# Where combination pieces and weight loads stand in the order of a gated S5 and dilated-attention block

## The chip, the core and the metric

The kernel runs on one core of one Trainium2 chip. The metric is the time of one execution in device microseconds, as the median of three runs. The engines are TensorE (PE for its matmuls, PEld for its weight loads), VectorE (DVE), ScalarE (ACT), GpSimd (POOL) and SyncE (SP); SP issues the DMAs that matter here, in one queue.

## The reference, cut to what matters

One layer on x of 2048 x 1024 in float32. A normalised h is multiplied by one wide matrix and split into the inputs of a state-space branch (u, z_s), queries, keys and values of 12 heads (3 groups of 4), a gate z_a, and two merge gates.

```python
proj = rmsnorm(x, pre_norm_g) @ w_in
u_s, z_s, q, k, v, z_a, g_s, g_a = split(proj)
y_s = s5_branch(u_s, ...) * silu(z_s)
# three groups (window, dilation) = (128,1), (512,4), (2048,16), four heads each
outs, lses = [dilated_group_attention(q_g, k_g, v_g) for g in range(3)]
alpha = softmax(lses over the three groups)      # per head slot j
y_a = sum(alpha * outs) * silu(z_a)
merged = sigmoid(g_s) * (y_s @ w_branch_s) + sigmoid(g_a) * (y_a @ w_branch_a)
x = x + rmsnorm(merged @ w_out, post_norm_g)
```

A head slot j has one head in each of the three groups. Its outputs are mixed by `alpha`, which needs the softmax sums of all three.

## The kernel before, in words

Every float32 operand of a large product is split into a rounded high part and a remainder (`split`: ACT writes the high part, DVE the low part), and a product is three matmuls (high x high, high x low, low x high). h lies split in on-chip memory for all of the first part of the program.

Weights come in pairs of 128-column strips. `pair` takes a pair of tiles from the pool `wp` (two pairs of buffers, so two pairs of strips can be held) and loads four parts of 256 KB through tiles of the tag `w_raw`, of which there are two. `proj` multiplies one strip with 512 columns of h in 24 matmuls: one bank.

The stages in order are: normalisation and the first products, the state-space branch with gate and value products beside it, the GLU, and then attention. Attention runs over four head slots j, and in each over three units, one for each group g (`unit`). A unit has one weight pair (query and key strip), and four chunks of 512 positions. A chunk projects keys and queries, loads its values from DRAM (tile `ev` for the banded groups g = 0 and 1, which ACT and DVE then split into `vh`, `vl`; tile `v` for g = 2, used as it comes), computes scores, softmax (tile `p`: DVE maximum, ACT exponential), transposes p on TensorE and multiplies with the values; the unnormalised result goes to DRAM (`numd`), the softmax sums go to `statd`.

After a slot's three units, `combine(j)` mixes its three outputs. It is a Python generator that is advanced one piece at a time beside later work. Its first piece loads the sums (`cm`), works out the three factors on DVE and ACT and stores them (`fd`). Then come eight pieces, one for each quarter and half: for each of the three groups a broadcast of the factor and a block of `numd` are loaded into one `w_raw` tile (there named `cnf`), GpSimd multiplies and adds them into the tile `cy`, and the sum goes to DRAM (`yad`). So combination and weight loads share the two `w_raw` tiles. GpSimd also copies two carried key blocks for each later chunk of a g = 0 unit.

Pieces of slot j are called for in slot j+1, after chunks 0, 1 and 3 of each unit (`if c != 2: next(beside, None)`), nine calls for nine pieces. Those of the last slot are called for after the banks of `emit(tanh(0), beside)` and `emit(tanh(2), beside)`, the first two pairs of merge-gate products. Then follow the z_a strips (`silu_pair`, whose results are multiplied by the combined output, loaded into `cy` tiles of the pool `za`) with `tanh(4)` between them, `tanh(6)`, and the loads of the first halves of both branch weights (`wbs`, `wba`), the first inputs of the last stage (`branch_inputs`) and its first gates. The last stage (`output`) runs over eight blocks of 256 positions: branch products (`br`), merge, output product (`po`), normalisation.

The program text isn't the order on the engines. [...] Tiles of one tag are handed out in the order of the text.

Of the kernel before, what the change touches and what calls it, by code (L numbers as in the profile page):

```python
# [11 lines left out]
F32 = mybir.dt.float32  # L12
# [27 lines left out]
class Builder:  # L40
# [783 lines left out]
    def unit(self, j, g, wp, pool, ev, psum, numd, statd, beside):  # L824
        nc = self.nc
        banded = g < 2
        w = self.pair(wp, IDX_Q + 4 * g + j, IDX_K + 4 * g + j)
        st = pool.tile([128, 2, 16], F32, name="st", bufs=2)
        prev = None
        for c in range(4):  # L830
            view = self.chunk(g, c)

            def project(s):
                ps = psum.tile([128, 512], F32, tag="proj", name="proj")
                self.proj(ps, w, s, view)
                return self.in_order(g, ps)

            vsrc = self.vd[g, 512 * c : 512 * c + 512, 128 * j : 128 * j + 128].rearrange("(b q) x -> q b x", b=4)
            pk = project(1)
            if banded:  # L840
                vh, vl = (pool.tile([128, 4, 128], F32R, name=n, bufs=2) for n in ("vh", "vl"))
                self.load_split(ev, "ev", vh, vl, vsrc)
                kh, kl = (pool.tile([128, 5, 128], F32R, name=n, bufs=2) for n in ("kh", "kl"))
                flat = lambda t: self.ordered(g, t.rearrange("p b i -> p (b i)"))
                self.split(flat(kh[:, 1:5]), flat(kl[:, 1:5]), pk)
                carry = g == 0 and c > 0
                if carry:
                    nc.gpsimd.tensor_copy(kh[:, 0], prev[0][:, 4])
                    nc.gpsimd.tensor_copy(kl[:, 0], prev[1][:, 4])
                pq = project(0)  # L850
                qh, ql = (pool.tile([128, 4, 128], F32R, name=n) for n in ("qh", "ql"))
                self.split(flat(qh), flat(ql), pq)
                self.banded_chunk(g, c, carry, qh, ql, kh, kl, vh, vl, prev, st, pool, ev, psum, numd[j, g, c])
                prev = (kh, kl, vh, vl)
            else:
                v = pool.tile([128, 4, 128], F32, tag="vh", name="v", bufs=2)
                nc.sync.dma_start(v, vsrc)
                k = pool.tile([128, 4, 128], F32, tag="kh", name="k", bufs=2)
                nc.scalar.activation(k.rearrange("p b i -> p (b i)"), pk, AF.Copy)
                pq = project(0)  # L860
                q = pool.tile([128, 4, 128], F32, tag="qh", name="q")
                nc.scalar.activation(q.rearrange("p b i -> p (b i)"), pq, AF.Copy)
                self.causal_chunk(c, q, k, v, st, pool, ev, psum, numd[j, g, c])
            if c != 2:
                next(beside, None)

        tp = psum.tile([32, 128], F32, tag="t", name="tst")
        nc.tensor.transpose(tp, st.rearrange("p s b -> p (s b)"), self.ident)
        sb = pool.tile([32, 128], F32, name="stt")
        if g == 0:  # L870
            nc.vector.tensor_copy(sb.rearrange("s (r i) -> s r i", r=16), tp.rearrange("s (i r) -> s r i", r=16))
            for s in range(2):
                nc.sync.dma_start(
                    statd[j, g, s].rearrange("(r b i) -> b r i", r=16, b=16),
                    sb[16 * s : 16 * s + 16].rearrange("s (r i) -> s r i", r=16),
                )
        elif g == 1:
            nc.vector.tensor_copy(sb.rearrange("s (m i) -> s m i", m=4), tp.rearrange("s (i m) -> s m i", m=4))
            for s in range(2):
                for c in range(4):  # L880
                    nc.sync.dma_start(
                        statd[j, g, s].rearrange("(m r b i) -> r b m i", m=4, r=4, b=4)[c],
                        sb[16 * s + 4 * c : 16 * s + 4 * c + 4].rearrange("s (m i) -> s m i", m=4),
                    )
        else:
            nc.vector.tensor_copy(sb, tp)
            nc.sync.dma_start(statd[j, g].rearrange("s (r i) -> (s r) i", r=16), sb)
# [102 lines left out]
    def combine(self, j, wp, pool, numd, statd, fd, yd):  # L990
# [2 lines left out]
        nc = self.nc  # L993
        m = pool.tile([128, 6, 16], F32, name="cm")
        nc.sync.dma_start(m, statd[j].rearrange("g s (p x) -> p (g s) x", x=16))
        mx = pool.tile([128, 16], F32, name="cx")
        nc.vector.tensor_tensor(mx, m[:, 0], m[:, 2], op=ALU.max)
        nc.vector.tensor_tensor(mx, mx, m[:, 4], op=ALU.max)
# [13 lines left out]
        for q in range(4):  # L1012
            for o in (0, 256):
                y = pool.tile([128, 256], F32, name="cy")
                for g in range(3):
                    r = wp.tile([128, 2, 256], F32, tag="w_raw", name="cnf", bufs=2)
                    f, n = r[:, 0], r[:, 1]
# [118 lines left out]
    def run(self, stop=None):  # L1136
        tc, nc, a = self.tc, self.nc, self.a
        with (
# [8 lines left out]
            ya = self.ya = dp.tile([4, 4, 128, 512], F32, name="ya")  # L1147
# [11 lines left out]
            T = dict(reuse_waits="tile")  # L1159
# [5 lines left out]
            with tc.tile_pool(name="w", bufs=2, **T) as wp, tc.tile_pool(name="ev", bufs=2, **T) as ev:  # L1165
# [37 lines left out]
                with tc.tile_pool(name="at", bufs=1, **T) as ap:  # L1203
                    self.mask = ap.tile([128, 256], F32, name="mask")
                    nc.sync.dma_start(self.mask, a["mask"])

                    beside = iter(())
                    for j in range(4):
                        for g in range(3):
                            self.unit(j, g, wp, ap, ev, psum, numd, statd, beside)  # L1210
                        beside = self.combine(j, wp, ap, numd, statd, fd, yad)
                    if stop == "att":
                        return

                    def tanh(c):
                        w = self.pair(wp, IDX_GA + c, IDX_GA + c + 1)
                        return self.tanh_pair(ev, psum, w, gta[c : c + 2])

                    def emit(banks, beside=iter(())):
                        for bank in banks:  # L1220
                            for step in bank:
                                step()
                            next(beside, None)

                    emit(tanh(0), beside)
                    emit(tanh(2), beside)
                with tc.tile_pool(name="za", bufs=1, **T) as zp:

                    def mixed(j, q):
                        f = zp.tile([128, 512], F32, name="cy", bufs=3)  # L1230
                        nc.sync.dma_start(f, yad[j, q])
                        return f

                    for p in range(2):
                        if p:
                            emit(tanh(4))
                        i = IDX_ZA + 2 * p
                        factor = [lambda q, j=j: mixed(j, q) for j in (2 * p, 2 * p + 1)]
                        emit(self.silu_pair(ev, psum, self.pair(wp, i, i + 1), ya[2 * p : 2 * p + 2], factor))
                if stop == "ya":  # L1240
                    return
                with tc.tile_pool(name="bs", bufs=1, **T) as bp:
                    emit(tanh(6))
                    wb = [self.weight(bp, wp, "w_raw", n, 4, (0, 512)) for n in ("wbs", "wba")]
                    first = self.branch_inputs(wp, 0, 256, ys, ya)
                    early = [bp.tile([128, 2, 256], F32, name="gt", bufs=2) for _ in range(2)]
                    for c, gt in enumerate(early):
                        self.gates(gt, c, 0)
                    hcm.__exit__(None, None, None)
                    with tc.tile_pool(name="out", bufs=1, side="right", **T) as op:  # L1250
                        self.output(op, bp, wp, ev, psum, wb, first, early, ys, ya, 256)
# [56 lines left out]
```

## Time and profile before

| | |
|---|---|
| Median of three runs | 2163.32 us (2162.99 to 2163.49) |
| The profiled execution's own time | 2165.62 us |
| Its span, first to last instruction | 2163.8 us |
| Mean granted TensorE clock | 0.983 |
| TensorE matmul busy | 2062.1 us, 95% of the span |
| VectorE, ScalarE, GpSimd busy | 41%, 27%, 19% of the span |
| HBM traffic | 106 GB/s over the span |

TensorE is the engine that is nearly always busy, so time is read from the stretches in which it is not, and from those in which its granted clock is below 1. The other engines matter where TensorE waits for them.

### The profile page before, as it was taken

The numbers are of one execution on the slowest core, as the hardware profiler recorded it, in microseconds if no ns is written. First come the engines' busy times: TensorE is split into PE (matmuls) and PEld (weight loads), VectorE is DVE, ScalarE is ACT, GpSimd is POOL, SyncE is SP. The second block draws the span as 40 slices with busy tenths as digits, with TensorE's granted clock in tenths as the row PEclk, the third lists the DMA queues.
The fourth block names the chain that finished last, engine by engine and source line by source line (L and its number), as shares of the span: only waits on it lengthen the run. The fifth ranks groups of instructions, "written<-read, shape, count | busy, mean of one in ns | idle before, by whom it ended". The sixth has DMA issues, their size and how long they took to land.

```text
span 2163.8 us, 31149 instructions
## 1 busy us (share of the span) xinstructions
PE 2062.1 (95%) x11668; PEld 1790.3 (83%) x11668; DVE 879.6 (41%) x2293; ACT 587.1 (27%) x1327; POOL 413.3 (19%) x464
## 2 busy tenths in 40 slices
PE   8999999999999999998998999899399999999998
PEld 6788888999999988876886787778378878899987
DVE  6981456555522244243323423341012125554435
ACT  6421122222223234232323323332021124211211
POOL 0002455555402100023003201300400001111111
PEclk9999999999999999999999999999799999999999
DMA  7333343343345411135115313421543247343323
GB/s 258 107 119 127 104 123 116 117 121 110 114 135 170 133 49 52 35 98 136 57 50 134 112 40 90 128 78 54 131 132 117 88 122 219 103 143 117 122 78 98
DMA packets 237239, 239.85 MB, mean 111 GB/s; under 512 B 48160, under 2 KB 177952, under 8 KB 236832
## 3 DMA queue, kind: packets, MB, share of 16 engines
q1 hardware_dynamic: 237088, 237.87, 36.5%
q8 instruction: 91, 1.49, 0.3%
q14 instruction: 60, 0.49, 0.1%
HBM read 150.65 MB, written 78.75 MB: 106 GB/s over the span
## 4 chain that ended last, share of the span: by engine, by line
PE 76%; DMA 13%; POOL 3%; DVE 3%; ACT 2%; issue 2%; SPq 1%; DVEq 0%; POOLq 0%; ACTq 0%
PE proj L141 40%; PE pv L163 12%; PE br L1092 7%; PE po L1111 7%; DMA cnf<-numd 4%; PE glu L786 2%; DMA w_raw<-in_wst_dram 2%; DMA yad<-cy 1%; DMA ev<-vd 1%; POOL cnf L1032 1%; DMA cnf<-fd 1%; POOL cy L1033 1%; PE s L917 1%; DMA raw<-in_wout_dram 1%; PE py L598 1%
## 5 line engine op out<-in xcount | busy, mean ns | idle before, releaser
L141 PE MATMUL proj<-hhi,w_hi 128*128 128x512 f32 x1664 | 665.6, 401 | 45.2 <-ACT w_hi L67 35.8
L141 PE MATMUL proj<-hlo,w_hi 128*128 128x512 f32 x1664 | 662.0, 398 | 3.8 <-DVE hlo L68 2.7
L141 PE MATMUL proj<-hhi,w_lo 128*128 128x512 f32 x1664 | 661.0, 398 | 0.0
L141 PEld LDWEIGHTS proj<-hhi,w_hi 128*128 128x128 f32 x1664 | 316.4, 190 | 115.3 <-ACT w_hi L67 36.3
L141 PEld LDWEIGHTS proj<-hlo,w_hi 128*128 128x128 f32 x1664 | 316.6, 190 | 72.5 <-DVE hlo L74 3.4
L141 PEld LDWEIGHTS proj<-hhi,w_lo 128*128 128x128 f32 x1664 | 316.4, 190 | 62.5
L163 PE MATMUL pv<-w_hi,hhi 128*128 128x256 f32 x768 | 218.8, 285 | 0.0
L163 PE MATMUL pv<-w_hi,hlo 128*128 128x256 f32 x768 | 214.5, 279 | 0.0
L163 PE MATMUL pv<-w_lo,hhi 128*128 128x256 f32 x768 | 214.5, 279 | 0.0
L68 DVE TENSOR_TENSOR w_lo<-w_raw,w_hi 128x512 fp32r<-128x512 f32 (+1 forms) x130 | 107.9, 848 | 256.0 <-ACT w_hi L67 255.5
L1095 POOL TENSOR_TENSOR gt<-gt 128x256 f32<-128x256 f32 x64 | 48.7, 764 | 504.9 <-DVE gt L1094 344.3
L163 PEld LDWEIGHTS pv<-w_hi,hhi 128*128 128x128 f32 x768 | 144.4, 188 | 0.6
L163 PEld LDWEIGHTS pv<-w_lo,hhi 128*128 128x128 f32 x768 | 144.4, 188 | 0.6
L163 PEld LDWEIGHTS pv<-w_hi,hlo 128*128 128x128 f32 x768 | 144.3, 188 | 0.0
L900 ACT ACTIVATE p<-p,nm 128x128 f32<-128x128 f32 (+1 forms) x192 | 87.2, 455 | 170.7 <-DVE nm L899 170.4
L67 ACT ACTIVATE w_hi<-w_raw 128x512 fp32r<-128x512 f32 (+1 forms) x130 | 77.9, 621 | 154.4 <-DMA w_raw<-in_wst_dram 123.0
L894 DVE CUSTOM_DVE_ANT_0 p<-s,mask 128x128 f32<-128x128 f32 (+1 forms) x192 | 64.8, 361 | 105.0 <-PE t L980 40.7
L1111 PE MATMUL po<-wout0h,mh 128*128 128x512 f32 x256 | 98.9, 392 | 2.4 <-ACT wout0h L67 2.4
L1111 PE MATMUL po<-wout0l,mh 128*128 128x512 f32 x256 | 99.8, 390 | 0.0
L1111 PE MATMUL po<-wout0h,ml 128*128 128x512 f32 x256 | 99.5, 390 | 0.0
L693 ACT ACTIVATE ge<-proj 128x512 f32<-128x512 f32 x64 | 38.0, 595 | 211.1 <-PE proj L141 174.7
L1094 DVE SCALAR_TENSOR_TENSOR gt<-gt,br 128x256 f32<-128x256 f32 x128 | 51.8, 418 | 68.9 <-PE br L1092 38.9
(249 smaller groups left out, 3295.4 us busy)
## 6 DMA issues: line engine op xcount, KB each, us to landing
w_raw<-in_wst_dram SPq DMA_DIRECT2D x126, 256.0 KB
vd<-ve SPq DMA_DIRECT2D x48, 256.0 KB
numd<-acc SPq DMA_DIRECT2D x48, 256.0 KB
cnf<-numd SPq DMA_DIRECT2D x96, 128.0 KB
cnf<-fd SPq DMA_DIRECT2D x96, 128.0 KB
xT<-in_xT_dram SPq DMA_DIRECT2D x32, 256.0 KB
gts<-ge SPq DMA_DIRECT2D x32, 256.0 KB
sx<-sx SPq DMA_DIRECT2D x64, 128.0 KB
```

What stands on the lines that cost most here:

```text
L67: nc.scalar.activation(hi, src, AF.Copy)
L68: nc.vector.tensor_tensor(lo, src, raw(hi), op=ALU.subtract)
L141: last = nc.tensor.matmul(ps, st[:, k, cs], m, start=n == 0, stop=n == 23)
L163: last = nc.tensor.matmul(ps[:, o], st[:, k, rs], m[:, k], start=n == 0, stop=n == 23)
L693: nc.scalar.activation(e, t["ps"], AF.Tanh, scale=0.5)
L786: nc.tensor.matmul(ps, st[:, k, cs], m[:, k], start=n == 0, stop=n == 11)
L894: nc.vector.tensor_tensor_reduce(p[:, :n], scores, mask, scale=1.0, scalar=-3.0e38, op0=ALU.add, op1=ALU.max, accum_out=st[:, 0, blk : blk ...
L900: nc.scalar.activation(p[:, :n], p[:, :n], AF.Exp, scale=HEAD_SCALE, bias=nm, accum_out=st[:, 1, blk : blk + 1])
L1092: nc.tensor.matmul(ps, st[:, k, cs], m[:, i, k], start=n == 0, stop=n == 11)
L1094: nc.vector.scalar_tensor_tensor(gt[:, i], gt[:, i], 1.0, ps, op0=ALU.add, op1=ALU.mult)
L1095: nc.gpsimd.tensor_tensor(gt[:, 0], gt[:, 0], gt[:, 1], op=ALU.add)
L1111: nc.tensor.matmul(po[b, half], st[:, k, bs], m[:, k, hs], start=k == 0 and n == 0, stop=k == 7 and n == 2,)
```

## The change

It has three parts.

1. In `unit`, the call that advances the combination moves from behind a chunk to before it, and is made for chunks 2 and 3 of the first unit and all four chunks of the second and the third. That is ten calls; `combine` gets one more `yield`, behind the load of the sums, so it has ten steps: load, factors, eight pieces. The calls of the second and third unit stand behind the load of that unit's weight pair.
2. Behind the last slot, both pairs of `tanh(0)` and `tanh(2)` are made (and their weights loaded) before any of their banks, and `emit` advances the combination before a bank, not behind it.
3. The pool `bs` is opened before the z_a strips. The combined output's tiles (`cy`) now take the two buffers of its tag `gt`, where they had three in a pool `za` of their own; the first halves of the branch weights are loaded between the load of the second z_a pair and its products, ahead of the weights of `tanh(6)`, where they were loaded behind `tanh(6)`.

```diff
         for c in range(4):
             view = self.chunk(g, c)
+            if g or c > 1:
+                next(beside, None)
...
                 self.causal_chunk(c, q, k, v, st, pool, ev, psum, numd[j, g, c])
-            if c != 2:
-                next(beside, None)
...
         nc.sync.dma_start(m, statd[j].rearrange("g s (p x) -> p (g s) x", x=16))
+        yield
         mx = pool.tile([128, 16], F32, name="cx")
...
                     def emit(banks, beside=iter(())):
                         for bank in banks:
+                            next(beside, None)
                             for step in bank:
                                 step()
-                            next(beside, None)
-
-                    emit(tanh(0), beside)
-                    emit(tanh(2), beside)
-                with tc.tile_pool(name="za", bufs=1, **T) as zp:
+
+                    for banks in (tanh(0), tanh(2)):
+                        emit(banks, beside)
+                with tc.tile_pool(name="bs", bufs=1, **T) as bp:
 
                     def mixed(j, q):
-                        f = zp.tile([128, 512], F32, name="cy", bufs=3)
+                        f = bp.tile([128, 512], F32, tag="gt", name="cy", bufs=2)
...
-                        emit(self.silu_pair(ev, psum, self.pair(wp, i, i + 1), ya[2 * p : 2 * p + 2], factor))
-                if stop == "ya":
-                    return
-                with tc.tile_pool(name="bs", bufs=1, **T) as bp:
+                        z = self.silu_pair(ev, psum, self.pair(wp, i, i + 1), ya[2 * p : 2 * p + 2], factor)
+                        if p:
+                            wb = [self.weight(bp, wp, "w_raw", n, 4, (0, 512)) for n in ("wbs", "wba")]
+                        emit(z)
+                    if stop == "ya":
+                        return
                     emit(tanh(6))
-                    wb = [self.weight(bp, wp, "w_raw", n, 4, (0, 512)) for n in ("wbs", "wba")]
                     first = self.branch_inputs(wp, 0, 256, ys, ya)
-                    early = [bp.tile([128, 2, 256], F32, name="gt", bufs=2) for _ in range(2)]
+                    early = [bp.tile([128, 2, 256], F32, tag="gt", name="gt", bufs=2) for _ in range(2)]
```

## Rows read from the trace of the kernel before

**Rows 1.** The page: TensorE's busy time, and its granted clock in 40 slices.
```profile
PE 2062.1 (95%) x11668; PEld 1790.3 (83%) x11668; DVE 879.6 (41%) x2293; ACT 587.1 (27%) x1327; POOL 413.3 (19%) x464
PEclk9999999999999999999999999999799999999999
```

**Rows 2.** TensorE's waits over the span: total us, times, longest us.
```profile
PE proj L141 <- ACT w_hi L67: 35.8, 1, 35.8
PE t L928 <- ACT p L900: 28.2, 16, 7.2
PE t L926 <- ACT p L900: 10.2, 3, 3.5
PE proj L141 <- ACT ge L693: 2.8, 2, 1.6
```

**Rows 3.** SP's queue behind the last slot: start us, us, line, names.
```profile
1436.39 0.38 SPq L1022 DMA_DIRECT2D cnf<-numd  x1
...
1507.08 0.37 SPq L1010 DMA_DIRECT2D fd<-ce  x1
...
1519.00 0.32 SPq L1034 DMA_DIRECT2D yad<-cy  x1
...
1527.94 0.32 SPq L1034 DMA_DIRECT2D yad<-cy  x1
...
1567.97 0.33 SPq L100 DMA_DIRECT2D w_raw<-in_wst_dram  x1
1569.94 0.32 SPq L1034 DMA_DIRECT2D yad<-cy  x1
...
1586.20 0.32 SPq L1034 DMA_DIRECT2D yad<-cy  x1
```

**Rows 4.** ScalarE's timeline around the same stretch, with the idle time before each.
```profile
1486.26 0.60 ACT L862 ACTIVATE q<-proj 128x512 f32<-128x512 f32 x1 [1.18 <-PE proj L141]
...
1570.87 0.63 ACT L67 ACTIVATE w_hi<-w_raw 128x512 fp32r<-128x512 f32 x1 [31.23 <-DMA w_raw<-in_wst_dram]
...
1587.82 0.63 ACT L67 ACTIVATE w_hi<-w_raw 128x512 fp32r<-128x512 f32 x1 [5.18 <-DMA w_raw<-in_wst_dram]
...
1590.09 0.63 ACT L67 ACTIVATE w_hi<-w_raw 128x512 fp32r<-128x512 f32 x1 [1.15 <-DMA w_raw<-in_wst_dram]
```

**Rows 5.** Windows after the hole: PE, PEld, DVE, ACT, POOL busy, PEclk, DMA share, GB/s.
```profile
1571.50:1575.00 3.50, 3.45 (x8) 2.78 (x9) 1.39 (x2) 0.63 (x1) 0.00 (x0) 0.50 0.48 146
1575.00:1580.00 5.00, 5.00 (x21) 4.02 (x21) 1.38 (x2) 1.26 (x2) 0.00 (x0) 0.88 0.40 105
...
1616.00:1660.00 44.00, 44.00 (x196) 36.43 (x195) 12.24 (x18) 6.98 (x12) 0.00 (x0) 1.00 0.35 111
```

**Rows 6.** Windows of attention units: first and third of slot 1, first of slot 3.
```profile
930.00:1009.00 79.00, 69.65 (x355) 56.62 (x354) 32.73 (x105) 28.46 (x73) 23.52 (x34) 0.98 0.48 124
...
1072.00:1122.00 50.00, 50.00 (x260) 41.72 (x259) 10.31 (x56) 13.02 (x42) 0.59 (x2) 1.00 0.13 42
...
1314.00:1397.00 83.00, 71.96 (x363) 58.53 (x362) 34.12 (x112) 29.43 (x76) 23.08 (x34) 0.94 0.45 119
```

**Rows 7.** SP's queue in slot 1's first unit.
```profile
933.67 0.36 SPq L1010 DMA_DIRECT2D fd<-ce  x1
...
951.51 0.33 SPq L100 DMA_DIRECT2D w_raw<-in_wst_dram  x1
...
959.86 0.33 SPq L1019 DMA_DIRECT2D cnf<-fd  x1
...
982.25 0.43 SPq L100 DMA_DIRECT2D ev<-vd  x1
```

**Rows 8.** ScalarE's and TensorE's timelines at the third chunk's wait in slot 1.
```profile
985.16 0.63 ACT L67 ACTIVATE vh<-ev 128x512 fp32r<-128x512 f32 x1 [11.20 <-DMA ev<-vd]
...
986.34 0.48 PE L928 MATMUL t<-ident,p 128*128 128x128 f32 x1 [5.53 <-ACT p L900]
```

**Rows 9.** Timeline under the last gate pair, where ScalarE splits branch inputs.
```profile
1776.89 0.50 PE L141 MATMUL proj<-hhi,w_hi 128*128 128x512 f32 x1 [1.59 <-ACT ge L693]
```

## The prediction

> **What bounds the kernel now.** I read the page first: TensorE is busy 95% of the span, and its clock is below full in one slice alone, the 29th of 40 [rows 1]. So the question is where its missing hundred microseconds lie, and the list of its waits answers it [rows 2]. One wait of 35.8 us stands for a single event: a projection that needs a freshly split weight tile. Nineteen waits, 28.2 + 10.2 = 38.4 us, are transposes that want the softmax's exponentials. Then a few small ones, of which 1.6 us matters here. The change touches all three kinds.
>
> The single hole is read from SP's queue and ScalarE's timeline. The last slot's factors are stored at 1507.08; its pieces end at 1519.00, 1527.94 and so on to the seventh at 1569.94, one per (1569.94 - 1519.00) / 6 = 8.49 us. The weights of the second gate pair stand behind the seventh piece in the order in which the two `w_raw` tiles are handed out, so their first load goes out at 1567.97 [rows 3]; ScalarE, idle for 31.23 us, splits it at 1570.87 [rows 4]. The first gate pair's eight banks are done at about 1535.7 (1570.87 + 0.63 + 0.04 of hand-over - 35.8). TensorE comes back at half its speed: clock 0.50 up to 1575, 0.88 in the next 5 us [rows 5].
>
> The softmax waits lie in first units and the start of second units of slots 1 to 3: in slot 1 the first unit leaves TensorE 79.00 - 69.65 = 9.4 us idle, the third nothing [rows 6]. The mechanism is in SP's queue. The value load of the fourth chunk is issued at 982.25, behind combination loads that wait for a tile [rows 7]; ScalarE, in order, sits 11.20 us before the split of those values, with the exponentials behind it, and the transpose waits 5.53 us [rows 8].
>
> **The change, part by part.**
>
> Part 2, the gate weights. In the new text order both gate pairs come before the last slot's pieces, and a tag's tiles go out in that order. The tile pair for the second is free when the last unit's projections end, 1486.26 [rows 4]; its four loads and splits need about as long as one pair took around 1570, some 8 us, so it is ready near 1497, 38 us before TensorE wants it. The hole closes: -35.8. The slow restart goes too: 8 + 21 = 29 matmuls took 8.5 us there, and at the pace of the steady stretch, 44 / 196 = 0.2245 us, they take 6.5 [rows 5]: -2.0.
>
> What is late next is the first z_a pair, which now stands behind the eighth piece. Eight pieces at 8.49 from the first end at 1519.00 + 7 x 8.49 = 1578.4, 7.8 us before the 1586.20 of before, which had the four weight loads inside it [rows 3]. The z_a splits move by as much: from 1587.82 to 1580.0 and from 1590.09 to 1582.3 [rows 4]. TensorE wants them at 1535.7 + 44 = 1579.7 [rows 5]. The first is written at 1580.6, 0.9 late; the second half of the strip adds some tenths. I take +1.5. The bounds are 0 and, if pieces take 10 us beside products (the first interval, with products beside it, is 8.94), 7 x 1.5 = 10.6 more. Sum of part 2: -35.8 - 2.0 + 1.5 = -36.3. The new splits near 1490 fall on a ScalarE and a VectorE with idle time there; if that cover is gone, four splits of 0.63 cost 2.5.
>
> Part 1, the pieces in attention. Here I don't take the text's order for the engine's. In the trace of before a piece's load from `numd` goes out at 1436.39, while its factors exist only at 1507.08 [rows 3]: the planner places a load as early as its tile allows. So the pieces will again start when the factors are there, about 934 in slot 1, in the first unit. What does change is the order on `w_raw`: the second unit's weight pair now stands ahead of the first piece, and can load while the slot before ends. In before its four loads take the queue from 951.51 to 959.86, 8.4 us, with pieces waiting on both sides [rows 7]. Of the 982.25 - 933.67 = 48.6 us from the factors to the longest-delayed value load that is 17%. If lateness falls in that proportion, 17% of 38.4 is -6.6. The bounds lie far apart. If the pieces really stay out of first units and the later ones cover them, all 38.4 go, and the clock's shares with them (0.02 x 79 = 1.6 us in slot 1's first unit, 0.06 x 83 = 5.0 in slot 3's [rows 6], some 10 in three slots): -48. If four pieces per unit delay as many value loads in the second unit as they now do in the first, nothing is gained, and up to three more waits of the middle size, 3.5 us [rows 2], come in: +10. I stay near the rows of before, since the same eight pieces pass through the same queue. The added `yield` issues nothing; the sums' load is the same DMA.
>
> A rule bears on this. In SP's rows a value load goes out only after the combination loads ahead of it in the queue, and ScalarE is idle for it meanwhile [rows 7, 8]. [...] By that rule the wait travels with the pieces, part 1 is worth 0, and the sum is 6.6 us higher.
>
> Part 3, the branch weights. Their eight loads leave the stretch under the last gate pair, where ScalarE's splits of the branch inputs made TensorE wait 1.59 us [rows 9]; the inputs can be split earlier: -1.6, with 0 as the other bound. The loads stand instead beside the second z_a pair, where TensorE is full and ScalarE is busy 6.98 of 44 us, VectorE 12.24 [rows 5]; eight splits add some 5 us to each: hidden, and 5 us if they were not. Two buffers in place of three for the combined output still leave a bank (44 / 8 = 5.5 us) to load one: nothing.
>
> Sum: -36.3 - 6.6 - 1.6 = -44.5. Against the profiled execution's own 2165.6 (span 2163.8 and 1.8 around it) that is 2121.1; the median of the runs lies 2.3 lower, so I forecast 2119.
>
> **Rivals.**
>
> The wait travels. Part 1 gives 0 to +10, the rest stands: 2125 to 2135. For it: the same eight pieces pass the same queue ahead of value loads that ScalarE has to split, and second units have those loads too.
>
> The pieces really leave the first units. Part 1 gives -20 to -48: 2077 to 2105. For it: the third unit has no wait and DMA is busy only 0.13 of its time [rows 6]. Against it: 1436.39.
>
> The hole moves to the z_a strip. At 10 us a piece it is 12 us wide: 2130. Against it: 8.49 and 8.94.
>
> The change doesn't do what it says: the second gate pair's loads still follow the pieces. Then only parts 1 and 3 are left: 2155. Against it: the `w_raw` tiles went out in text order at every place I read.
>
> Slower. The place is the second and third units, where eight pieces now have eight chunks: if every chunk there waits, the 24 waits must sum to 38.4 + 37.9 = 76.3 us to eat the gain, 3.2 us each. The mean today is 38.4 / 19 = 2.0. At the longest of today, 7.2 us [rows 2], it is 173 us and 2163 + 97 = 2260. From 3.4 us a chunk on the kernel is slower than before.
>
> **How the numbers follow.** The forecast has 0.44 (its own range 2109 to 2125), the travelling wait 0.25, empty first units 0.17, a hole at z_a 0.07, a hole that stays 0.04, slower 0.03. The range of 8 in 10 reaches over the travelling wait and most of the z_a case at the top and half of the empty-units case at the bottom: 2092 to 2136. About 0.2% (4 us) is what a measurement of this kernel can tell from no change. Faster takes all but the last case and a sliver between: 0.96; same 0.01; slower 0.03.
>
> **What the profile after would show.** Right: no wait of `proj` for `w_hi` over 3 us; the second gate pair's splits near 1490; full clock through the stretch; factors stored as early in a slot as before, and pieces running in the first unit; softmax waits of 25 to 38 us in sum; no wait for `ge` near the last gate pair's end. The prediction is wrong if pieces start only in second units, if softmax waits sum to under 20 or over 48 us, or if `proj` waits for z_a weights by more than a few microseconds.

## The result and the profile after

The changed kernel takes 2134.61 us, the median of four runs (2132.93 to 2138.11), against 2163.15 for the kernel before: a ratio of 0.9872 with a 95% interval of 0.9855 to 0.9889. That is 28.5 us faster, where 44 were forecast (2119). The profiled execution took 2132.93 us, with a span of 2131.1, so profile against profile it is 2163.8 - 2131.1 = 32.7 us faster. Its mean granted clock is 0.989.

The page, TensorE's busy time and its granted clock in 40 slices. One slice is still low, with an 8 where [rows 1] has a 7:

```profile
PE 2063.0 (97%) x11668; PEld 1793.6 (84%) x11668; DVE 875.5 (41%) x2293; ACT 586.6 (28%) x1327; POOL 413.6 (19%) x464
PEclk9999999999999999999999999999989999999999
```

TensorE's waits in the changed kernel (total us, times, longest us), to be read against [rows 2]:

```profile
PE proj L141 <- ACT ge L693: 18.5, 4, 13.5
PE t L926 <- ACT p L900: 7.8, 3, 3.4
...
PE proj L141 <- DVE kl L68: 6.3, 3, 2.4
PE s L917 <- ACT qh L67: 6.3, 3, 2.6
PE na L946 <- DVE acc L966: 4.6, 2, 3.1
...
PE t L928 <- ACT p L900: 0.9, 4, 0.3
...
PE po L1112 <- ACT wout0h L67: 0.4, 2, 0.3
```

The 35.8 us for `w_hi` are gone from the list. The exponentials are down from 38.4 to 8.7 us, but three names are new beside them, `kl`, `qh` and `acc`: all are in the same attention units, so the attention waits are 7.8 + 0.9 + 6.3 + 6.3 + 4.6 = 25.9, and 26.2 with one of 0.3 for `ph`. And the wait for `ge`, the tanh eviction that empties a gate bank, has grown from 2.8 to 18.5, with a single one of 13.5. That is where the missing part of the gain went.

ScalarE's timeline at that wait (start us, us, instruction, idle time before it and what ended it):

```profile
1541.48 0.60 ACT L693 ACTIVATE ge<-proj 128x512 f32<-128x512 f32 x1 [7.37 <-DMA gta<-ge]
1550.82 0.60 ACT L693 ACTIVATE ge<-proj 128x512 f32<-128x512 f32 x1 [8.74 <-DMA gta<-ge]
1556.60 0.60 ACT L693 ACTIVATE ge<-proj 128x512 f32<-128x512 f32 x1 [5.18 <-DMA gta<-ge]
1568.84 0.63 ACT L67 ACTIVATE w_hi<-w_raw 128x512 fp32r<-128x512 f32 x1 [11.64 <-DMA w_raw<-in_wst_dram]
1574.05 0.63 ACT L67 ACTIVATE w_hi<-w_raw 128x512 fp32r<-128x512 f32 x1 [4.58 <-DMA w_raw<-in_wst_dram]
1575.37 0.63 ACT L67 ACTIVATE w_hi<-w_raw 128x512 fp32r<-128x512 f32 x1 [0.70 <-DMA w_raw<-in_wst_dram]
1575.91 0.58 ACT L693 ACTIVATE ge<-proj 128x512 f32<-128x512 f32 x1
```

TensorE's timeline at the same place:

```profile
1542.13 0.50 PE L141 MATMUL proj<-hhi,w_hi 128*128 128x512 f32 x1 [1.84 <-ACT ge L693]
...
1551.47 0.50 PE L141 MATMUL proj<-hhi,w_hi 128*128 128x512 f32 x1 [1.99 <-ACT ge L693]
...
1576.54 0.80 PE L141 MATMUL proj<-hhi,w_hi 128*128 128x512 f32 x1 [13.54 <-ACT ge L693]
```

SP's queue behind the last slot, as in [rows 3]:

```profile
1507.08 0.32 SPq L1035 DMA_DIRECT2D yad<-cy  x1
...
1560.25 0.32 SPq L1035 DMA_DIRECT2D yad<-cy  x1
...
1561.63 0.41 SPq L699 DMA_DIRECT2D gta<-ge  x1
...
1565.96 0.33 SPq L100 DMA_DIRECT2D w_raw<-in_wst_dram  x1
1568.73 0.32 SPq L1035 DMA_DIRECT2D yad<-cy  x1
```

These three are read together. Twelve of the sixteen gate banks are evicted by 1557.2. The next instruction in ScalarE's queue isn't the thirteenth eviction but the first split of the z_a weights, and those weights stand behind the eighth piece in SP's queue: the first of their four loads goes out at 1565.96. ScalarE stands 11.64 us before that split, and 4.58 and 0.70 before the next two; only then, at 1575.91, comes the thirteenth eviction. TensorE has gate weights and work, fills the two product banks that it has (48 matmuls from 1551.47 on), and stops at 1563.00 for 13.54 us. The pieces are hardly slower than thought (8.49): (1568.73 - 1507.08) / 7 = 8.81 us each. The 1.84 and 1.99 us are a smaller form: ScalarE idles up to 8.74 us for an output tile, whose store (`gta`) stands between pieces in SP's queue.

Windows of the stop and the restart (columns as in [rows 5]):

```profile
1562.90:1576.00 13.10, 0.10 (x1) 0.00 (x0) 1.38 (x2) 1.88 (x4) 2.90 (x5) 0.67 0.60 181
1576.00:1579.50 3.50, 2.96 (x7) 2.38 (x8) 1.39 (x2) 1.60 (x4) 0.00 (x0) 0.50 0.71 213
1579.50:1584.50 5.00, 5.00 (x20) 4.00 (x20) 0.00 (x0) 0.07 (x1) 0.00 (x0) 0.86 0.39 113
```

The restart at half clock is back with the new stop: 7 + 20 = 27 matmuls take 7.96 us, and at 0.2245 each [rows 5] they would take 6.06.

SP's queue in slot 1's first unit and the start of the second, as in [rows 7]:

```profile
938.90 0.36 SPq L1011 DMA_DIRECT2D fd<-ce  x1
...
950.00 0.33 SPq L1035 DMA_DIRECT2D yad<-cy  x1
...
966.62 0.50 SPq L100 DMA_DIRECT2D ev<-vd  x1
...
975.97 0.34 SPq L100 DMA_DIRECT2D w_raw<-in_wst_dram  x1
```

The pieces still begin in the first unit, whatever the text says; the first is stored at 950.00. The weight pair that had stood among them [rows 7] is loaded before them, two of its four loads at 862 and two at 913; what is loaded at 975.97 is already the third unit's. The value load that ScalarE waits for longest is now the third chunk's, which goes out at 966.62: 8.66 us of idle time end in front of its `vh`, with the `kh` eviction right behind it: hence the new name `kl`. The fourth chunk's, the longest-delayed of before, goes out at 983.23 and costs ScalarE 0.16.

How long ScalarE stands before all value splits (the view of the tile `ev`: us, times), in the kernel before, in the changed one, and in the one below in which GpSimd issues the pieces:

```profile
  DMA ev<-vd: 88.7, 16
  DMA yad<-cy: 13.1, 2
...
  DMA ev<-vd: 84.1, 15
...
  DMA ev<-vd: 7.0, 8
```

The first two lines are the kernel before: 101.8 us in sum. So the change took 17% of this idle time away, while TensorE's waits in attention fell by 12.2 of 38.4, or 32%.

### The profile page after: what moved, and what is told of

It reads as the page before. It is cut to its first block, busy times and chain, and to the rows that moved or that the text cites. A ratio compares the mean times of both kernels' runs of the same rounds, so it can differ in the third digit from the quotient of the medians.

```text
span 2131.1 us, 31162 instructions
## 1 busy us (share of the span) xinstructions
PE 2063.0 (97%) x11668; PEld 1793.6 (84%) x11668; DVE 875.5 (41%) x2293; ACT 586.6 (28%) x1327; POOL 413.6 (19%) x464
## 3 DMA queue, kind: packets, MB, share of 16 engines
q1 hardware_dynamic: 237088, 237.87, 37.0%
## 4 chain that ended last, share of the span: by engine, by line
PE 77%; DMA 14%; POOL 3%; DVE 2%; ACT 1%; issue 1%; SPq 1%; POOLq 0%; DVEq 0%; ACTq 0%
PE proj L141 41%; PE pv L163 13%; PE br L1093 7%; PE po L1112 7%; DMA cnf<-numd 5%; DMA yad<-cy 2%; PE glu L786 2%; DMA w_raw<-in_wst_dram 1%; POOL cnf L1033 1%; POOL cy L1034 1%; PE s L917 1%; POOL cy L1026 1%; DMA cnf<-fd 1%; DMA raw<-in_wout_dram 1%; PE py L598 1%
## 5 line engine op out<-in xcount | busy, mean ns | idle before, releaser
L141 PE MATMUL proj<-hhi,w_hi 128*128 128x512 f32 x1664 | 666.9, 401 | 31.7 <-ACT ge L693 18.5
L141 PEld LDWEIGHTS proj<-hhi,w_hi 128*128 128x128 f32 x1664 | 316.1, 190 | 101.8 <-ACT ge L693 20.4
L1096 POOL TENSOR_TENSOR gt<-gt 128x256 f32<-128x256 f32 x64 | 48.4, 758 | 489.9 <-DVE gt L1095 328.6
```

What stands on the lines that cost most here:

```text
L141: last = nc.tensor.matmul(ps, st[:, k, cs], m, start=n == 0, stop=n == 23)
L1096: nc.gpsimd.tensor_tensor(gt[:, 0], gt[:, 0], gt[:, 1], op=ALU.add)
```

## Experiments

In the diffs, lines are against the kernel before or against the changed one, as said. Every ratio is against runs of the kernel before that were taken beside it.

**Each part alone.** Part 1, against before (the added call takes the tenth step):

```diff
+            if g or c > 1:
+                next(beside, None)
...
-            if c != 2:
-                next(beside, None)
...
+        yield
...
+                    next(beside, None)
                     emit(tanh(0), beside)
```

> Part 1 alone on the kernel before (the calls move to chunks 2 and 3 of the first unit and all of the second and third, with the extra step; the last slot's first step is called once ahead of the first gate pair, so that its pieces stand as before). Theory: the gain in attention comes from the second unit's weight pair standing ahead of the first piece, and is independent of the rest: softmax and neighbouring waits of slots 1 to 3 fall from 38.4 us to about 26, the 35.8 us hole stays: 2147 to 2152 us. Rival, that attention gained only through what the other parts moved: waits stay at 38 us, 2161 to 2165.

2153.88 us, 0.9945 (0.9928 to 0.9961): 0.55%, 12 us. The attention waits are 25 us, under the new names, and the hole for `w_hi` stays at 33.2.

Part 2, against before:

```diff
+                            next(beside, None)
                             for step in bank:
                                 step()
-                            next(beside, None)
...
-                    emit(tanh(0), beside)
-                    emit(tanh(2), beside)
+                    for banks in (tanh(0), tanh(2)):
+                        emit(banks, beside)
```

> Part 2 alone (both gate pairs' weights ahead of the last slot's pieces). Theory: the 35.8 us wait for the second gate pair's weights goes and a wait of some 13.5 us before the first z_a strip takes its place, with ScalarE idle 11 to 12 us in front of a weight split that stands ahead of evictions in its queue: net 35.8 + 2 - 17 = 20 gained, 2141 to 2146 us. Rival, that the new hole comes from the two combined-output buffers or the early branch weights of part 3: no hole here, 2126 to 2130 us.

2148.14 us, 0.9917 (0.9903 to 0.9932): 18 us. Its waits of TensorE show the exchange in pure form, with the attention waits untouched:

```profile
PE t L928 <- ACT p L900: 29.3, 12, 7.1
PE proj L141 <- ACT ge L693: 19.1, 5, 12.8
PE t L926 <- ACT p L900: 8.4, 3, 3.4
```

The `ge` hole needs neither part 1 nor part 3.

Part 3, against before:

```diff
-                with tc.tile_pool(name="za", bufs=1, **T) as zp:
+                with tc.tile_pool(name="bs", bufs=1, **T) as bp:
...
-                        f = zp.tile([128, 512], F32, name="cy", bufs=3)
+                        f = bp.tile([128, 512], F32, tag="gt", name="cy", bufs=2)
...
+                        if p:
+                            wb = [self.weight(bp, wp, "w_raw", n, 4, (0, 512)) for n in ("wbs", "wba")]
```

> Part 3 alone (branch weights beside the second z_a pair, two buffers for the combined output). Theory: the 1.6 us wait for an eviction under the last gate pair and some 2 us of waits for output weights in the first block go: 2158 to 2161 us. Rival, nothing or a loss, because two buffers delay the z_a evictions: 2163 or more, with new waits in the z_a strips.

2162.76 us, 0.9993 (0.9982 to 1.0004): not told from no change. The wait under the last gate pair is gone, another of 1.4 us has come, and the wait for output weights is 1.4 in place of 2.4. The three parts alone sum to 0.55 + 0.83 + 0.07 = 1.45%; together they give 1.28%.

**Is it the order on ScalarE that costs 13.5 us?** Against the changed kernel, the z_a splits are tied behind the fourteenth gate eviction, and nothing else:

```diff
+                        else:
+                            with tc.issue_after(self.evicts[-3].ins):
+                                w = self.pair(wp, i, i + 1)
```

> The changed kernel, with one edge in ScalarE's queue: the splits of the first z_a pair stand behind the eviction of the sixth bank of the second gate pair (the planner put them behind the fourth). No data or load moves. Theory (the hole is ScalarE's order): TensorE runs the last two gate banks (11 us) while the z_a load is under way, the hole of 13.5 us falls below 3 and its slow restart goes: 2119 to 2123 us. Rival (SP's queue, pieces and stores are late, so the z_a weights would be waited for anyway, or evictions wait for output buffers): the hole stays over 8 us, 2129 to 2135.

2127.91 us, 0.9825 (0.9811 to 0.984). ScalarE's timeline with the tie:

```profile
1567.93 0.60 ACT L694 ACTIVATE ge<-proj 128x512 f32<-128x512 f32 x1 [8.04 <-PE proj L142]
1573.98 0.60 ACT L694 ACTIVATE ge<-proj 128x512 f32<-128x512 f32 x1 [5.46 <-DMA gta<-ge]
1574.48 0.62 ACT L68 ACTIVATE w_hi<-w_raw 128x512 fp32r<-128x512 f32 x1
```

The split comes behind the evictions and has nothing to wait for, and no wait for `ge` is longer than 4.1. The weights' first load goes out at 1568.59, no earlier than the 1565.96 of the changed kernel. So the order was the cause of the large hole. But seven waits, 9.4 us in sum, are left; at the longest ScalarE is idle 9.28 us for a `gta` store. The time falls between the two expectations, because both causes are real.

**Is it only that the z_a weights are late?** Against the changed kernel, that pair is traced ahead of the second gate pair's banks (behind six pieces, and in a second kernel behind four):

```diff
-                    for banks in (tanh(0), tanh(2)):
-                        emit(banks, beside)
+                    first, second = tanh(0), tanh(2)
+                    emit(first, beside)
+                    wz = self.pair(wp, IDX_ZA, IDX_ZA + 1)
+                    emit(second, beside)
```

> The changed kernel, with the first z_a pair's weights traced between the banks of the first and the second gate pair, that is behind six pieces, with two pieces after it. Theory (the hole before z_a is one of order, the z_a weights behind eight pieces): the hole goes as it does with the edge in ScalarE's queue, since nobody needs the last two pieces before the second z_a pair: 2120 to 2128 us, the waits for evictions under 10 us in sum. Rival (the stretch is limited by the pieces' own transfers and stores in SP's queue): the hole shrinks but the evictions wait for output buffers instead, over 12 us in sum, 2129 to 2135.

> The changed kernel, with the first z_a pair's weights traced behind four pieces, pieces still on SP's queue. Theory (the hole is the number of pieces ahead of these weights against the banks that TensorE has left): the wait before z_a goes, eviction waits in sum under 6 us, 2114 to 2122. Rival (ScalarE's order lets the weights' wait block evictions wherever they stand): a hole of 8 us or more, as behind six pieces, 2122 to 2128.

Behind six: 2123.55 us, 0.9817 (0.98 to 0.9833). Behind four: 2130.97, 0.9825 (0.9807 to 0.9843). The first time lies where the theory had it, and the second lies above what either view expected, though its ratio is the tied kernel's, since the kernel before took 2168.41 beside it. But neither kernel took the hole away: 10.7 us is the longest wait for `ge` in the first, 9.6 in the second, whose ScalarE shows the same picture 27 us earlier:

```profile
1526.77 0.60 ACT L693 ACTIVATE ge<-proj 128x512 f32<-128x512 f32 x1 [5.54 <-DMA gta<-ge]
1542.11 0.63 ACT L67 ACTIVATE w_hi<-w_raw 128x512 fp32r<-128x512 f32 x1 [14.74 <-DMA w_raw<-in_wst_dram]
...
1545.04 0.58 ACT L693 ACTIVATE ge<-proj 128x512 f32<-128x512 f32 x1
```

In all three places that were tried (behind eight, six and four pieces) the weight load is late, and its split stands ahead of evictions: ScalarE stands 11.64, 17.23 and 14.74 us before it, and the next eviction starts behind it, at 1575.91, 1549.15 and 1545.04. The simple theory of late weights fell here.

**Where do 12 us in attention come from?** Against before, the first three calls move behind the second unit's weight pair, and the first unit's calls go; the rest of part 1 is left out:

```diff
+            if g == 1 and c == 0:
+                for _ in range(3):
+                    next(beside, None)
...
-            if c != 2:
+            if g and c != 2:
```

> The kernel before, with the first pieces traced behind the second unit's weight pair and nothing else moved: the order on the shared tiles is pair, five pieces, pair, three pieces, where it was two pieces, pair, three pieces, pair, three pieces. Theory (part 1 gains because that pair leaves the chain of pieces): most of part 1's gain, waits of slots 1 to 3 from 38 to 24 to 32 us, 2150 to 2157. Rival (part 1 gains through where its calls stand, four pieces and then the third unit's pair): less than 3 us, 2161 to 2165.

2156.65 us, 0.9971 (0.9961 to 0.9981): 0.29% against part 1's 0.55%, about half, though the two intervals leave room from a quarter to all. The traces say more: TensorE's waits in attention are 10.1 + 6.9 + 5.9 + 5.6 + 0.5 = 29.0, where part 1 alone has 25.0 and the kernel before 38.4, so 9.4 of 13.4 us; and ScalarE's idle time before value splits is 85.1 against part 1's 85.6. So the value loads get earlier by that weight pair alone, and with it most of the gain comes; why the same lateness costs TensorE 4 us less in part 1 is not shown.

**What if pieces really ran only in second and third units?** Against the changed kernel, each load of a piece is tied behind the store of the chunk before its call:

```diff
-                    nc.sync.dma_start(f, fd[j, g : g + 1, at : at + 256].to_broadcast([128, 256]))
+                    with self.tc.issue_after(behind):
+                        nc.sync.dma_start(f, fd[j, g : g + 1, at : at + 256].to_broadcast([128, 256]))
```

> The changed kernel, with an edge in SP's queue from the store of the chunk before to every load of a piece, so that pieces run where the text calls for them: beside second and third units alone. Theory (the wait travels with the pieces): the waits of first units go, those of the second unit grow to 2 to 4 us a chunk, the sum over three slots stays between 18 and 32 us: 2128 to 2140. Rival (first units were the trouble, later units hide the pieces): the sum falls under 8 us, 2108 to 2120.

2250.95 us, 1.0406 (1.0391 to 1.0422). Both expectations were wrong by more than 100 us. TensorE's waits:

```profile
PE proj L141 <- ACT w_hi L67: 90.3, 6, 17.5
PE t L926 <- ACT p L900: 21.2, 7, 6.4
```

SP's queue from the end of slot 1's first unit to the start of its third:

```profile
995.09 0.43 SPq L1022 DMA_DIRECT2D cnf<-fd  x1
...
1056.27 0.34 SPq L1040 DMA_DIRECT2D yad<-cy  x1
1056.66 0.92 SPq L100 DMA_DIRECT2D w_raw<-in_wst_dram  x2
```

ScalarE and TensorE at the same place:

```profile
1059.65 1.27 ACT L67 ACTIVATE w_hi<-w_raw 128x512 fp32r<-128x512 f32 x2 [9.02 <-DMA w_raw<-in_wst_dram]
...
1064.24 0.79 PE L141 MATMUL proj<-hhi,w_hi 128*128 128x512 f32 x1 [14.07 <-ACT w_hi L67]
```

The pieces do stay out of the first unit (the first starts at 995.09, behind the first unit's last store). But the third unit's weights stand behind the second unit's pieces on the two shared tiles, and go out only when the last of these is stored. That makes three of the six waits (14.07 here, 41.9 us in three slots). The other three, 48.4 us, come after third units: there the pair that follows (the next slot's first, or a gate pair) stands behind the third unit's pieces in the same way. So the changed kernel depends on pieces not running where the text puts them. Staging tiles of their own for the pieces would part the two chains; that wasn't tried.

**Is it SP's queue?** Here the pieces' loads and stores are issued by GpSimd, with the same tiles, first on the changed kernel and then on before:

```diff
-                    nc.sync.dma_start(f, fd[j, g : g + 1, at : at + 256].to_broadcast([128, 256]))
+                    nc.gpsimd.dma_start(f, fd[j, g : g + 1, at : at + 256].to_broadcast([128, 256]))
...
-                nc.sync.dma_start(yd[j, q][:, o : o + 256], y)
+                nc.gpsimd.dma_start(yd[j, q][:, o : o + 256], y)
```

> The changed kernel, with the pieces' loads and their stores issued by GpSimd and not by SP; order on the tiles unchanged. Theory (value loads and gate stores are late because they stand behind the pieces' waits in SP's queue): waits of slots 1 to 3 fall from 26 to under 10 us and evictions no longer wait for output buffers; the split of the z_a weights ahead of evictions may stay: 2105 to 2122. Rival (the two shared tiles or the transfers themselves are the limit): waits stay over 20 us, 2130 to 2140; or GpSimd issues so slowly that pieces get longer and the hole before z_a grows: over 2140.

> The kernel before, with the pieces' loads and stores issued by GpSimd and nothing else changed. Theory: attention's waits (38 us) go without any of the change, the wait for the second gate pair's weights stays and grows by the slower pieces (10.5 us in place of 8.5, seven of them): 50 us, 2118 to 2135. Rival (the change's order is needed for attention too): waits of slots 1 to 3 stay over 15 us, 2140 or more.

On the changed kernel: 2091.09 us, 0.9668 (0.9652 to 0.9684). On before: 2125.49 us, 0.9801 (0.978 to 0.9821). In both, none of the attention waits counted above is left in TensorE's list; on before, the wait for the second gate pair's weights is still there and has grown from 35.8 to 49.8 us. Windows of slot 1's first and second unit on the changed kernel with GpSimd issuing; in [rows 6] the first has 69.65 busy:

```profile
930.00:1009.00 79.00, 79.00 (x435) 67.39 (x434) 37.79 (x131) 32.67 (x86) 41.99 (x67) 1.00 0.47 112
1009.00:1072.00 63.00, 63.00 (x333) 53.49 (x332) 22.19 (x85) 22.66 (x65) 21.40 (x33) 1.00 0.40 108
```

The DMA share is as high as before (0.48 there), so the traffic beside the unit was not the cause: the place of the waits was. ScalarE's idle time before value splits says the same: 7.0 us here, where the changed kernel has 84.1. The edit does more than change the issuer: the page lists these 29.37 MB under another DMA queue, in 10752 packets, where the queue of SP's transfers loses 237088 - 188448 = 48640. The packets' time didn't fall for it (32.0 + 6.7 = 38.7% of the span, against 37.0%), and in [rows 7] the value load is late already when it is issued, so lighter traffic doesn't explain the gain. SP's other transfers don't keep their places either (in slot 1 the third unit's first weight load goes out at 979.78 here, 0.69 us behind a `numd` store, and at 975.97 in the changed kernel, 0.39 us ahead of one), so this is shown of the queue, not of a single load. What is left is one wait, and its cause on ScalarE:

```profile
PE proj L141 <- ACT w_hi L67: 14.1, 1, 14.1
```

```profile
1526.44 0.60 ACT L693 ACTIVATE ge<-proj 128x512 f32<-128x512 f32 x1 [4.84 <-PE proj L141]
1539.74 0.63 ACT L67 ACTIVATE w_hi<-w_raw 128x512 fp32r<-128x512 f32 x1 [12.70 <-DMA w_raw<-in_wst_dram]
```

All gate banks are done by then, and the z_a weights stand behind the eighth piece: the plain form of the late pair that the prediction had in mind.

**Can that last one be closed?** With GpSimd issuing, the z_a pair goes behind four pieces, as above; then also the third gate pair's splits are tied behind the fifth z_a eviction:

```diff
+                            with tc.issue_after(self.evicts[-4].ins):
+                                third = tanh(4)
+                            emit(third)
```

> The changed kernel with the pieces' transfers issued by GpSimd, and the first z_a pair's weights traced behind four pieces, between the banks of the two gate pairs. Theory (two separate causes: SP's queue in attention, the order on the shared tiles behind it): no waits in slots 1 to 3 and none before z_a; the 14.1 us wait left with GpSimd's queue and its slow restart go: 2071 to 2080 us. Rival (the wait travels to the next pair, that of the third gate pair, which now follows the pieces): a wait of 5 to 14 us there, 2083 to 2092.

> The run before it with GpSimd's queue and z_a behind four pieces, plus one edge in ScalarE's queue: the splits of the third gate pair's weights stand behind the eviction of the fifth bank of the first z_a pair. No load moves. Theory (a weight split that waits at the head of ScalarE's queue, ahead of evictions, makes the hole, and not the weights' lateness itself): the 15.0 us wait goes with its slow restart, no wait over 3 us behind the last slot, 16 to 18 us less than that run, 0.955 to 0.958 of the kernel before. Rival (the weights are late for TensorE anyway): a wait for them of 8 us or more takes its place, 0.960 to 0.964.

Behind four: 2087.73 us, 0.963 (0.9612 to 0.9647), and a wait of 15.0 for `ze` is the only large one: the wait travelled to the third gate pair, whose split held ScalarE for 13.00 us. With the tie: 2084.33 us, 0.9643 (0.963 to 0.9656), not told from the other by ratio. ScalarE then shows:

```profile
1556.28 0.60 ACT L694 ACTIVATE ze<-proj 128x512 f32<-128x512 f32 x1 [19.32 <-DMA ya<-ze]
```

A hole of 10.5 us stays, and the theory of a single cause fell: the z_a results also wait for the combined output. The chain that ended last, at this place (start us, us):

```profile
1548.72 0.73 POOL cy L1035
...
1549.46 0.33 SPq L101
...
1549.85 3.55 DMA cy<-yad
```

The last piece gives up its shared tile, the weight load that waited for it goes out (L101), and only behind that, in SP's queue, does the load of the combined output. It doesn't wait for the last piece's store, which GpSimd begins to issue at 1549.73. So a load that waits for a tile still holds another that doesn't need it, now with a weight load in the pieces' place. These two are the fastest versions found, 3.6 to 3.7% below the kernel before.

## Why the prediction was right, and where it wasn't

The likeliest case had the right direction and, but for the z_a pair and the size of the gain in attention, the right mechanism. The time lies in the range, but in its upper part, above the forecast's own 2109 to 2125, and in part by luck: the z_a pair and the restart came out 15.9 + 1.9 = 17.8 us dearer than forecast, attention and the output weights 5.6 + 2.0 = 7.6 cheaper. It also lies in the 2125 to 2135 of the travelling wait, but by number alone: that rival has part 1 at 0 or a loss, and part 1 alone gave 12 us. Term by term, profile against profile:

| Term | Forecast | Measured |
|---|---|---|
| Hole for the second gate pair | -35.8 | -35.8 |
| Slow restart behind it | -2.0 | -0.1 (1.9 come back with the new hole) |
| z_a pair late | +1.5 | +17.4 (13.54 + 1.99 + 1.84, all for `ge`) |
| Attention waits | -6.6 | -12.2 (38.4 to 26.2) |
| Part 3 | -1.6 | -1.6, and -2.0 on output weights; alone not told from 0 |
| Sum | -44.5 | -34.3, where the spans differ by 32.7 |

- **The gate weights.** Right: the second pair is split from 1473.9 to 1479.5, and no wait for `w_hi` is left. The forecast had 1490; attention ends some 11 us sooner.
- **The z_a pair, +1.5: the step that failed.** It named the right transfer as next and had the pieces' pace right (8.81 us, where 8.49 was taken). It put the cost at the moment when TensorE wants those weights. But ScalarE stood before the first split from the end of the twelfth eviction on, 11.64 us, and four gate evictions stood behind it. TensorE lost its banks before it lost its weights. The tied kernel shows it: the 13.5 us go while the weights come no earlier. The sign of full clock through the stretch failed with this step, and the sign of a wait for z_a weights didn't show it, since the wait was for `ge`. The rival of a hole at the z_a strip had nearly the size, 12 us, but by pieces of 10 us: size by chance, mechanism not. The 3.8 us of small waits are gate stores behind pieces in SP's queue, which no part of the working named.
- **The attention waits, -6.6.** The mechanism was right: pieces still start in the first unit, and the second unit's weight pair leaves their chain. The 17% was right for the lateness itself: ScalarE's idle time before value splits fell from 101.8 to 84.1. The step from there to TensorE's waits in the same proportion was mis-sized: they fell by 32%, twice as much. The kernel with that pair moved has the same idle time on ScalarE and 9.4 of the 13.4 us that part 1 takes off TensorE's waits; the rest stays open. By the letter one of its own signs of being wrong came up: the waits for exponentials are 8.7 us, under its 20. They had changed names, because the late value load now stands before `kh` and the third unit's splits before `qh`.
- **The rule that waits travel with the pieces** held in its mechanism and not in its price of 0. Moving the pieces' calls, still on SP's queue, gave 0.55%; taking them out of it gave about 2%.
- **Part 3, -1.6.** Right in place, and too small to be seen alone.
- **Slower.** The price for it lay elsewhere than I put it. Pieces kept in second and third units cost 21.2 us by the exponentials (7.8 in the changed kernel), and 90.3 us by the next unit's weights. Its break-even is 76.3 / 24 = 3.2 us a chunk; the 3.4 named there follows only if the 4 us of noise are added.

## What to carry to other kernels

When a load is moved, look up what stands behind its first consumer in that consumer's queue: here a weight split for which ScalarE stood 11.64 us held four gate evictions behind it, and TensorE stopped 13.54 us for banks with its weights in place. Where one queue issues both long waiting chains and loads that others need soon, give the chain a queue of its own before tuning its order; here that was worth more than the whole change, with either order (about 2% against 1.28%). And read from the trace where the moved work really runs: the text said second and third units, the first piece of slot 1 was stored at 950.00 in the first, and doing what the text says cost 116 us.

## What the runs showed of the hardware

Transfers issued by GpSimd were dearer one by one: 224 of them add 548.2 - 413.6 = 134.6 us of busy time, 0.60 us each, where SP's rows above show mostly 0.32 to 0.50 for one issue, and a piece behind the last slot takes (1539.86 - 1509.06) / 3 = 10.3 us in place of 8.81. The kernel is 44 us faster all the same (0.9872 to 0.9668 of 2163), since value loads and gate stores no longer stand behind them. The stop of 13.5 us was followed by a granted clock of 0.50 and then 0.86, as the one of 35.8 was by 0.50 and 0.88 [rows 5]: the shorter stop cost as slow a restart, 1.9 us against 2.0.
